# One wait per pair of write-backs, and the last store's wait in a section of its own: a row maximum over NaN data on one core

## The chip, the cores and the metric

The kernel runs on one core of one Trainium2 chip. The metric is the device time of a whole execution in microseconds (us); lower is better. The profile's span is some 1.8 us shorter than that time.

## The reference

```python
def setup_inputs():
    batch, seq, dim = 32, 2048, 2048
    x = np.random.randn(batch, seq, dim).astype(np.float32)
    mask = np.random.rand(batch, seq, dim) < 0.1
    x[mask] = np.nan
    return {"x": x, "axis": -1}

def reference(x, axis):
    return np.nanmax(x, axis=axis).astype(np.float32)
```

536.87 MB go in, 65,536 row maxima come out. A tenth of the elements are NaN and must not count.

## The kernel before

SyncE loads tiles of up to seven rows per partition into three large buffers. For each piece of a tile, ScalarE makes a 16-bit key from the upper half of every float (`kt`), a key in which NaN sorts low. GpSimd, or for a few pieces ScalarE (the negative numbers in `TILES`), writes the key back over the upper half (`xt`). VectorE then reduces whole rows with `tensor_reduce`. Each engine has a semaphore that it raises once per instruction, and `Order.add` works out which of them an instruction has to wait for. Where there are several, all but the last become wait instructions of their own:

```python
    def add(self, who, engine, issue, deps, lane=None, step=1):
        want = self.needed(who, deps)
        for s, v in want[:-1]:
            engine.wait_ge(self.sems[s], v)        # a separate wait instruction
        inst = issue()
        for s, v in want[-1:]:
            inst._wait_ge(self.sems[s], v)         # the wait on the instruction
        ...
# in the loop over the pieces of a tile:
                        if back:                   # ScalarE writes this piece back
                            held.append((at - c, at, key, kp, e_key))
                            ...
                        else:                      # GpSimd does
                            e = pool([e_key], out=to, in0=kp, scalar1=-1.0, ...)
                            kfree[key].append(e)
                            clean.append((at - c, at, e))
                        while reds and done + reds[0] <= ...:
                            ...
                            e = dve([e for a, b, e in clean if b > lo and a < done] + part,
                                    nc.vector.tensor_reduce, ...)
# ... at the end, inside the one critical section that holds the whole kernel:
        for (og, bits), e in zip(stores, ready):
            last = order.add("sp", nc.sync, lambda: nc.sync.dma_start(out=og, in_=bits), [e], ...)
        nc.sync.wait_ge(order.sems[last[0]], last[1])
```

The last tile, number 74 by the kernel's count, is cut into nine loads and seven maxima of one row each, so that little work is left after the last load.

## Time and profile before

| | before |
|---|---|
| time, median of the first three runs | 1253.67 us |
| span | 1251.8 us |
| read from HBM | 536.87 MB, 429 GB/s over the span |
| busy share: VectorE, GpSimd, ScalarE | 89%, 93%, 79% |
| separate waits on VectorE | 18 |
| last store landed to end of span | 1.28 us |

The prediction below shows the lines of the page, of a table of windows, of the chain of waits and of the source lines. In the table of windows the columns are the stretch, its length, the busy time of the engines with counts of instructions, the clock, the share of the 16 DMA engines' time that was busy, and GB/s.

### The profile page before, as it was taken

What the parts mean: (1) busy time and instruction counts of PE and PEld (TensorE: products, weight loads), DVE (VectorE), ACT (ScalarE), POOL (GpSimd) and SP (SyncE); (2) the same over time, 40 slices, a digit from 0 to 9 for tenths busy, and PEclk for the clock granted to TensorE, in tenths of its full rate; (3) what the DMA queues carried; (4) which work ended last, traced back from release to release, by engine and by line L of the source; (5) the groups of instructions that cost most, each with busy time, mean ns of one, the idle gap of its engine ahead of it and who ended that gap; (6) DMA issues with size and microseconds to landing.
All of it is one profiled execution on the core that took longest, in us unless ns stands there. A gap on an engine that the chain in (4) does not pass through costs nothing.

```text
span 1251.8 us, 892 instructions
## 1 busy us (share of the span) xinstructions
DVE 1110.9 (89%) x181; ACT 986.9 (79%) x273; POOL 1168.4 (93%) x242
## 2 busy tenths in 40 slices
DVE  0788989888889988898988888998888899999998
ACT  3777887778787877788777877777777878999998
POOL 2999989998999899998999899999999999989997
DMA  9999999999999999999999999999999999999997
GB/s 415 436 418 436 440 440 436 422 433 440 440 434 423 433 440 440 436 425 429 440 440 438 425 427 440 440 438 429 423 440 440 435 434 421 437 428 431 431 428 288
DMA packets 15991, 537.20 MB, mean 429 GB/s; under 512 B 2544, under 2 KB 2544, under 8 KB 3568
## 3 DMA queue, kind: packets, MB, share of 16 engines
q1 hardware_dynamic: 15984, 537.14, 99.3%
q14 instruction: 7, 0.06, 0.0%
HBM read 536.87 MB, written 0.26 MB: 429 GB/s over the span
## 4 chain that ended last, share of the span: by engine, by line
DMA 36%; DVE 33%; POOL 19%; ACT 10%; SPq 1%; issue 1%; DVEq 0%
DMA xt<-in_x_dram 36%; DVE acc L195 33%; POOL xt L191 19%; ACT kt L187 9%; ACT xt L187 1%; SPq L253 1%; DVE none L201 0%; DVE acc L215 0%; SPq L411 0%; DVEq L124 0%; SPq L183 0%
## 5 line engine op out<-in xcount | busy, mean ns | idle before, releaser
L191 POOL TENSOR_SCALAR xt<-kt 128x3584 int16<-128x3584 uint16 (+11 forms) x236 | 1167.4, 4946 | 78.5 <-ACT kt L187 60.3
L195 DVE TENSOR_REDUCE acc<-xt 128x3 f32<-128x6144 f32 (+4 forms) x175 | 1107.7, 6380 | 137.1 <-POOL xt L191 129.2
L187 ACT ACTIVATE kt<-xt,scalars 128x3584 uint16<-128x3584 int16 (+9 forms) x247 | 935.5, 3825 | 257.8 <-DMA xt<-in_x_dram 241.8
L187 ACT ACTIVATE xt<-kt 128x512 int16<-128x512 uint16 (+6 forms) x24 | 52.8, 2200 | 0.7
L187 ACT ACT_TABLE_LOAD x1 | 1.3, 1283 | 0.9 <-SPq L183 0.9
L195 DVE TENSOR_REDUCE xt<-xt 128x1 f32<-128x1536 f32 x1 | 1.7, 1742 | 0.0
L221 DVE MEMSET scalars<- 128x1 f32 x1 | 0.1, 59 | 1.0 <-SPq L183 1.0
L201 DVE TENSOR_SCALAR none<-acc 128x414 int32<-128x414 f32 (+1 forms) x2 | 0.8, 380 | 0.1
L215 DVE TENSOR_TENSOR acc<-acc,none 128x414 int32<-128x414 int32 (+1 forms) x2 | 0.7, 374 | 0.1
L201 POOL TENSOR_SCALAR late<-acc 128x91 int32<-128x91 f32 x1 | 0.5, 545 | 0.1
L215 POOL TENSOR_TENSOR acc<-acc,late 128x91 int32<-128x91 int32 x1 | 0.3, 343 | 0.1
L397 POOL MEMSET const-float32-0.0<- 128x1 f32 x1 | 0.1, 98 | 0.2 <-issue 0.2
L187 ACT ACTIVATE scalars<-scalars 128x1 f32<-128x1 f32 x1 | 0.2, 203 | 0.0
L397 POOL MEMSET const-uint8-127<- 128x1 uint8 x1 | 0.1, 102 | 0.0
L397 POOL MEMSET const-bfloat16-1.0<- 128x1 bf16 x1 | 0.1, 101 | 0.0
L397 POOL MEMSET const-float32-1.0<- 128x1 f32 x1 | 0.1, 98 | 0.0
## 6 DMA issues: line engine op xcount, KB each, us to landing
xt<-in_x_dram SPq DMA_DIRECT2D x61, 7168.0 KB, 22.5
xt<-in_x_dram SPq DMA_DIRECT2D x2, 5120.0 KB, 17.3
xt<-in_x_dram SPq DMA_DIRECT2D x3, 2816.0 KB, 22.5
xt<-in_x_dram SPq DMA_DIRECT2D x4, 2048.0 KB, 22.1
xt<-in_x_dram SPq DMA_DIRECT2D x5, 1536.0 KB, 28.9
xt<-in_x_dram SPq DMA_DIRECT2D x2, 3584.0 KB, 24.5
xt<-in_x_dram SPq DMA_DIRECT2D x6, 1024.0 KB, 26.7
xt<-in_x_dram SPq DMA_DIRECT2D x3, 1792.0 KB, 29.8
```

The lines of the kernel that those rows point to most:

```text
L187: return order.add("act", nc.scalar, lambda: nc.scalar.activation(**kw), deps)
L191: "pool", nc.gpsimd, lambda: nc.gpsimd.tensor_scalar(**kw), deps
L195: return order.add("dve", nc.vector, lambda: do(**kw), deps)
L201: lambda: engine.tensor_scalar(out=none, in0=acc, scalar1=NONE, scalar2=float(0x00800000), op0=ALU.is_equal, op1=ALU.mult,),
L215: lambda: engine.tensor_tensor(out=bits, in0=bits, in1=none, op=op),
L221: e_top = order.add("dve", nc.vector, lambda: nc.vector.memset(top, EDGE), [])
L253: lambda: nc.sync.dma_start(out=xt[:, at : at + c], in_=xg[:, base + at : base + at + c]),
L397: nc = _bacc.Bacc("TRN2", target_bir_lowering=False, num_devices=1)
```

## The change

There are two intents. First, where a maximum needs a write-back of GpSimd and one of ScalarE last, both raise one semaphore of that pair, and VectorE waits once. Second, the wait for the last store goes to a critical section that only SyncE enters, so that the engines' closing round runs while the store is in flight.

```diff
+APART = (70, 71, 72, 73)
+def joints(pieces, reds):
+    ...                      # which pieces are the last two, one of each engine, of a maximum
 ...
         inst.then_inc(self.sem(name), step)
 ...
+        past = self.past.get((name, event[1] - step), {}) if joint else {}
 ...
-        def pool(deps, **kw):
+        def pool(deps, pair=None, **kw):
             return order.add(
-                "pool", nc.gpsimd, lambda: nc.gpsimd.tensor_scalar(**kw), deps
+                "pool", nc.gpsimd, lambda: nc.gpsimd.tensor_scalar(**kw), deps,
+                lane=pair, joint=pair is not None,
             )
 ...
+                if number not in APART:
+                    pairs = joints(pieces, [n // Q for n in reds])
 ...
+                def cleaned(a, b, k, i, e):     # a piece counts when both of its pair are done
+                    ...
 ...
+    with tc.tile_critical():
         nc.sync.wait_ge(order.sems[last[0]], last[1])
```

(The same is done for `act`. `APART` lists four tiles that are left as they were.) In the built program VectorE's separate waits go from 18 to 8, ScalarE's from 14 to 18, and SyncE gains a few at the end.

## The prediction

> **What bounds the kernel now.** I read the page first, then a table of windows over the last fifth, then the chain of waits, and last the source lines of the two kinds of wait that change. From the page:
>
> ```profile
> span 1251.8 us, 892 instructions
> ...
> DVE 1110.9 (89%) x181; ACT 986.9 (79%) x273; POOL 1168.4 (93%) x242
> ...
> DMA  9999999999999999999999999999999999999997
> ...
> HBM read 536.87 MB, written 0.26 MB: 429 GB/s over the span
> ```
>
> All three compute engines are busy, but only the DMA row is full from the first slice to the 39th: 536.87 MB have to be read, and the span is mostly the time of that. The page's chain gives DVE 33% and GpSimd 19%; that is no contradiction, since a load is issued when VectorE frees a buffer and then waits in a queue that is already full. The windows over the last fifth show it (window, its length, busy us of VectorE, ScalarE, GpSimd with counts, clock, DMA share, GB/s):
>
> ```profile
> 1060.00:1140.00 80.00, 79.93 (x14) 76.85 (x25) 73.03 (x16) 1.00 0.99 429
> 1140.00:1200.00 60.00, 59.97 (x18) 57.05 (x24) 57.50 (x19) 1.00 1.01 431
> 1200.00:1235.00 35.00, 34.97 (x18) 33.67 (x24) 33.31 (x17) 1.00 1.01 425
> 1235.00:1240.00 5.00, 4.50 (x3) 4.92 (x4) 3.89 (x4) 1.00 1.02 425
> 1240.00:1245.00 5.00, 5.00 (x3) 4.94 (x6) 4.67 (x5) 1.00 0.41 146
> 1245.00:1252.00 7.00, 4.04 (x4) 1.28 (x2) 2.21 (x3) 1.00 0.04 7
> ```
>
> The DMA share stays at about 1.0 until 1240 although VectorE is also at 79.93 of 80 us. So a reduction that starts a little earlier before 1240 frees a buffer a little earlier for a transfer that only queues longer. After 1240 the loads are over (by the trace's records the last lands at 1243.20), and the end is set by this stretch of the chain of waits (start us, us, what):
>
> ```profile
> 1213.18 23.03 DMA xt<-in_x_dram
> ...
> 1236.24 1.58 ACT kt L187
> 1237.82 0.07 issue
> 1237.89 1.92 POOL xt L191
> 1239.81 0.03 issue
> 1239.84 2.01 DVE acc L195
> 1241.84 0.20 issue
> 1242.04 2.06 DVE acc L195
> ...
> 1244.23 2.15 DVE acc L195
> ...
> 1246.42 2.29 DVE acc L195
> ```
>
> A load lands at 1236.21, is turned into keys, written back, and the fourth row maximum of the last tile starts at 1239.84. From there four maxima follow back to back, starting 2.20, 2.19 and 2.19 us apart, though the intervals have waits of pairs in them. The waits themselves:
>
> ```profile
> L124 DVEq EVENT_SEMAPHORE  x18: 21/21/21, 158.1 to 1246.4; - x18
> ...
> L183 SPq COMPARE_BRANCH  x1: 38/38/38, 1250.5 to 1250.5; - x1
> ...
> L183 POOLq DRAIN  x1: 41/41/41, 1250.8 to 1250.8; - x1
> L183 DVEq DRAIN  x1: 17/17/17, 1250.8 to 1250.8; - x1
> ...
> L183 SPq NOP  x1: 18/18/18, 1251.0 to 1251.0; - x1
> ```
>
> The first line is the extra wait instruction that VectorE runs before a maximum that needs two engines: 18 in the whole kernel. The others are the round at the end: SyncE branches 0.02 us after the last store has landed (1250.53), then ScalarE, GpSimd and VectorE drain, and SyncE collects their answers until its NOP at 1251.02.
>
> **What the skill says.** The Trainium skill, "Perfetto Trace Analysis", section "Identifying Dependency Chains": an instruction that waits for several engines may have EventSemaphore instructions put before it. The trace agrees: 18 of them on VectorE. The same page, "Per-instruction lifecycle", under "DVE / Act Engine Instruction": an instruction with its own wait stands in a hardware wait queue, pushed there ahead of time, while under "Sequencer-only Instruction" the sequencer fetches the next one only after its own wait is over. So a separate wait should cost something only when it is the last to be met. The trace agrees. The third maximum of the last tile starts 110 ns after GpSimd's end (1236.938 to 1237.048) through the separate wait, the fourth 35 ns after it (1239.801 to 1239.836) with the wait on itself: a late separate wait costs about 75 ns. On DMA, "DMA: Bandwidth & Descriptors", section "Anatomy of one DMA", says that the fixed cost is mostly the write receipt before the semaphore; here the last store, 3.5 KB, takes 1.40 us from issue to landing (1249.13 to 1250.53), and neither kernel can shorten that.
>
> **The change, part by part.** The order of instructions on each engine shows that no computation and no transfer moves. What moves:
>
> *Pairs.* In ten maxima (tiles, counted from 1, 9, 17, 25, 33, 41, 63, 66, 67, 68 and the fifth of the last tile) the two waits become one, on a semaphore that both write-backs raise; VectorE's separate waits go from 18 to 8. In three more maxima of the last tile (third, sixth, seventh) the separate wait stays, but is for an earlier piece. ScalarE gains four waits (14 to 18), in tiles 63, 66, 67 and 68. The upper bound is 13 times 75 ns, 0.98 us, if every one were late and on the path. They are not:
> - In the five early tiles the maximum waits up to 1.6 us for ScalarE's write-back, a wait that stands on the instruction itself already; the separate one, for GpSimd, is met 0.4 us before the start (in the one at 293.83, the wait was over at 293.42). Gain 0.
> - Tile 63: separate wait ends at 1065.295, start 1065.339, 68 ns after the maximum before had ended. Gain up to 0.07 us on VectorE, but the DMA queue is full then, and VectorE has 0.50 us of idle time later, before 1239.84, that is set by a landing. Gain at the end 0.
> - Tiles 67 and 68: separate waits end 0.40 and 1.48 us before the start. Gain 0.
> - Last tile: the third maximum could start 44 ns earlier (back to back would be 1234.811 + 2.193 = 1237.004), and this vanishes in the same 0.50 us. The fifth starts 2.203 us after the fourth where plain neighbours are 2.193 apart: 0.01 us, and this one counts. The sixth and seventh are 2.192 and 2.193 apart: 0, but they can follow the fifth, as their last write-back ends at 1246.317, over 0.1 us before the start at 1246.424.
> Sum at the end: 0.01 us.
>
> *The last wait.* In before, landing to SyncE's arrival at the closing barrier takes 1250.528 to 1251.157, 0.63 us: branch, the semaphore for the others, three drains, two collecting waits, a NOP, a drain. In the changed kernel the round with the three engines follows the issue of the store and lies inside its 1.06 us of flight (1249.465 to 1250.528); it needed 0.45 us (1250.583 to 1251.034). But the second section brings its own: after the landing a wait, a branch, a semaphore, a drain that waits for it, a NOP that waits for the drain, and the closing drains, all on SyncE. From intervals of before, as an estimate: wait seen 0.017 and run 0.028, step to the branch 0.044, branch 0.038, step after it 0.127, semaphore 0.017, step 0.074, drain 0.007, step 0.060, NOP 0.018, step 0.044, drain 0.007, step 0.056: sum 0.54 us. Saved: 0.63 - 0.54 = 0.09 us. The barrier after it has the same instructions.
>
> Total 0.01 + 0.09 = 0.10 us: 1253.67 - 0.10 = 1253.57, given as 1253.55.
>
> **Rivals.** (1) *The whole round is saved.* If the second section's own steps are mostly merged or run ahead, all of 0.45 us goes: 1253.2. For it: branches without a wait are not seen in the trace at all, so some steps may vanish. Against: the second section's branch carries a wait, and such a branch was seen, with 0.127 us after it. (2) *The new section takes the place of the old.* If the added instructions at the end have to be fetched anew, or each step costs more than in before, the end is 0.1 to 0.3 us later: 1253.8 to 1254.0. For it: more waits and another branch on SyncE. Against: most of them run during the store's flight. (3) *The pairs matter upstream.* If an earlier release of a buffer shortened the loading, up to 1 us could go: 1252.6. For it: VectorE is at 100% from 1060 on. Against: the DMA share of 0.99 to 1.01 there, and loads that land 17 us or more after their issue. (4) *ScalarE's four new waits hurt:* at most 4 x 0.075 = 0.3 us in tiles 63 to 68. ScalarE is at 76.85 of 80 us there, so it has room, and the 0.50 us at 1239.3 would swallow the rest.
>
> **Range and chances.** The three runs of before lie 0.2 us apart, which is twice the expected gain, so the measured difference may come out as nothing. Rival 1 sets the lower end at about 1253.15, rival 2 and drift between runs the upper at about 1253.95. Two per cent is 25 us; nothing here touches that, so within 2% gets 0.99.
>
> **What would show it.** Right: VectorE's separate waits 8 in place of 18 and ScalarE's 18 in place of 14; busy times of the engines and the loads' landings as before within their noise; the last four maxima 2.19 us apart; from the last store's landing to the end of the span about 1.19 us where before has 1.28 (1251.81 - 1250.53). Wrong: the load before the fourth last maximum landing at clearly another time than 1236.2, which would make loading the cause; landing to end shortened by 0.3 us or more (rival 1), or lengthened (rival 2).

## More of the kernel before

One line that the prediction did not show turns out to matter. It is in the list of DMA queues between 1225 and 1245 us (queue and kind: packets, MB, share of 16 engines):

```profile
q1 hardware_dynamic: 1812, 7.06, 86.2%
q14 instruction: 1, 0.01, 0.1%
```

Beside the 1812 packets of loads and stores, one packet of 8 KB carries instructions. Over the whole span there are seven such packets.

## The result

The changed kernel took 1253.16 us (median of six runs, 1253.02 to 1253.23) against 1253.72 us for the kernel before (six runs, 1253.66 to 1253.86), so 0.56 us less. The ratio is 0.9995. Ratios are the mean time of one kernel's runs over that of the other's of the same rounds, so not quite the ratio of the medians. The 95% interval, 0.9982 to 1.0008, holds 1. The six times of the one do not overlap the six of the other, and in two later sessions the same kernel came out 0.75 and 0.71 us under before. A gain of 0.5 to 0.75 us is therefore real, but it is 0.05% of the time.

The page of the changed kernel:

```profile
span 1251.3 us, 893 instructions
...
DVE 1110.9 (89%) x181; ACT 986.8 (79%) x273; POOL 1169.5 (93%) x242
...
DMA  9999999999999999999999999999999999999997
...
HBM read 536.87 MB, written 0.26 MB: 429 GB/s over the span
```

Busy times and the DMA row are those of before. The windows at the end, with the same columns:

```profile
1235.00:1240.00 5.00, 5.00 (x4) 5.00 (x4) 4.62 (x4) 1.00 1.02 426
1240.00:1245.00 5.00, 5.00 (x3) 4.93 (x6) 4.68 (x5) 1.00 0.39 136
1245.00:1252.00 7.00, 3.61 (x4) 0.77 (x1) 1.70 (x3) 1.00 0.04 8
```

VectorE is busy for all 5.00 us between 1235 and 1240, where before it was for 4.50. The half microsecond of idle time ahead of the fourth-last maximum is gone. The timeline of VectorE shows the same, first of before, then of the changed kernel (start us, us, engine and line, operation, shape, count, and in brackets the idle time before it and what ended it):

```profile
1239.84 8.87 DVE L195 TENSOR_REDUCE acc<-xt 128x1 f32<-128x2048 f32 x4 [0.50 <-POOL xt L191]
```

```profile
1232.81 15.47 DVE L243 TENSOR_REDUCE acc<-xt 128x1 f32<-128x2048 f32 x7
```

Before, the last four maxima are a group of their own behind a gap; now all seven of the last tile are one group. The chain of waits of the changed kernel agrees (start us, us, what):

```profile
1235.86 1.34 POOL xt L236
1237.20 0.02 issue
1237.22 5.54 DVE acc L243 x3
1242.77 1.04 issue
```

It no longer goes through a landing at 1236.21. By the trace's records the load in question now lands at 1235.64, 0.57 us earlier, although the loads up to 1230 land 0.19 us later than before. The change of 0.75 us happens at one load: a 512 KB load that landed 1.98 us after its predecessor now lands 1.23 us after it. It was not issued earlier (at 1210.47 in place of 1210.28), so an earlier release of its buffer is not the reason. The fourth-last maximum starts at 1239.43 in place of 1239.84, and the last store lands at 1250.13 in place of 1250.53.

What sits in that place is the packet of instructions. The DMA queues of the changed kernel, first between 1225 and 1245 us (where before had two kinds of packets), then between 1245 and the end:

```profile
q1 hardware_dynamic: 1808, 7.03, 85.6%
```

```profile
q1 hardware_dynamic: 288, 0.05, 3.7%
q14 instruction: 1, 0.01, 0.3%
```

The trace's records put the packet at 1231.70 us before and at 1245.62 us now. The last load lands at 1243.06, so the packet now comes after all of them.

The source lines of the waits, as the prediction showed them for before:

```profile
L158 DVEq EVENT_SEMAPHORE  x8: 21/21/21, 1181.6 to 1244.4; - x8
...
L219 SPq NOP  x1: 18/18/18, 1249.4 to 1249.4; - x1
...
L493 SPq EVENT_SEMAPHORE  x5: 17/17/464, 1249.6 to 1251.2; - x5
...
L493 SPq COMPARE_BRANCH  x1: 38/38/38, 1250.2 to 1250.2; - x1
```

VectorE has 8 separate waits. SyncE's round with the others ends with its NOP at 1249.4, during the store's flight, where before it ended at 1251.0. From the landing (1250.13) to the end of the span (1251.28) it is 1.15 us, where before had 1.28.

So the 0.53 us of the two profiled spans (1251.81 and 1251.28) are 0.13 us at the end and 0.40 us in the landing of the last store, and the latter come from a load.

### The profile page after: what moved, and what is told of

It is laid out like the page before. It is cut to its first block, busy times and chain, and to the rows that moved or that the text cites. A ratio compares the mean times of both kernels' runs of the same rounds, so it can differ in the third digit from the quotient of the medians.

```text
span 1251.3 us, 893 instructions
## 1 busy us (share of the span) xinstructions
DVE 1110.9 (89%) x181; ACT 986.8 (79%) x273; POOL 1169.5 (93%) x242
## 4 chain that ended last, share of the span: by engine, by line
DMA 38%; DVE 27%; POOL 20%; ACT 13%; issue 1%; SPq 0%; ACTq 0%
DMA xt<-in_x_dram 38%; DVE acc L243 27%; POOL xt L236 20%; ACT kt L226 11%; ACT xt L226 2%; SPq L307 0%; DVE none L249 0%; DVE acc L263 0%; SPq L493 0%; ACTq L158 0%; SPq L219 0%
```

## The theories

**Fetch theory.** VectorE's program is fetched in blocks as it runs. Ten wait instructions fewer put the last fetch of that stream behind the last load in place of among the last loads, and the loads are no longer held up by it. The Trainium skill, "Runtime: NRT & Kernel Launch", section "Instruction fetch mechanics", says that each sequencer fetches its next page by DMA while it executes the current one, and calls the cost mostly hidden; "DMA: Bandwidth & Descriptors", section "Queues, rings and completion order", gives queue row 14 to the runtime's own traffic, refills among it. The trace agrees with the mechanism: seven packets of 8 KB on queue 14 in both kernels. By "Perfetto Trace Analysis", section "The 4-stage abstract model", an instruction has 64 bytes; as an estimate from that, one packet is 128 instructions. ScalarE had started 48 and 175 instructions at two of the packets of before, GpSimd 52 and 180 at two others: 127 and 128 apart. VectorE had started 189 at the last packet in both kernels, at 1231.70 and at 1245.62. Its other packet does not show the same step: by these counts it comes 133 instructions before the last one in before (56 at 434.2 us) and 142 in the changed kernel (47 at 385.7). So the count alone does not lay the packet to VectorE's stream, and the trace does not name its owner; the experiments have to.

**Wait theory.** The separate waits themselves were late and held up the maxima; with fewer of them VectorE, and through it the loads, run earlier.

**Section theory.** The end section alone makes the gain.

## The experiments

In all of them the result was correct. Times are medians of five runs, "before" is the kernel before in the same rounds (nine runs). Each call used one chip, and before's medians differ between them by up to 0.25 us, so only differences within a call are compared. The intervals of the ratios (about plus or minus 0.13%, 1.6 us) are wider than all these differences; what is read are medians that hang together over runs, and the traces. The five runs of one version lie 0.2 to 1.0 us apart, so a difference of 0.1 or 0.2 us between medians is not resolved. The profiled run is one of the five and not always a typical one: for pairs alone and for six waits it was the fastest, for the section alone and for nine waits the slowest. Starts of maxima are therefore not compared across versions to the tenth; what is compared is what happens inside a trace.

### The two parts alone

Pairs alone: the changed kernel without its second section.

```diff
-
-    with tc.tile_critical():
         nc.sync.wait_ge(order.sems[last[0]], last[1])
```

> The change without its second section: pairs alone, the last store's wait back where it was. Fetch theory (the pairs take ten instructions from VectorE's stream, so that its last instruction fetch falls after the last load in place of among the last loads): the 8 KB packet on the instruction queue is at about 1245.6 us, the fourth-last maximum starts near 1239.4, saving about 0.42 us: 1253.30. Section theory (the end alone accounts for it): no saving, 1253.72. Landing of the last store to the end of the span as before, 1.28 us.

Measured: 1253.30 us against 1253.66, 0.36 less (single runs 1252.95 to 1253.39). The packet is at 1245.4, there is no gap before the fourth-last maximum, which starts at 1239.18, and landing to end is 1.28 us. The section theory falls as the whole explanation.

The section alone: the kernel before with the one line `with tc.tile_critical():` added.

```diff
+
+    with tc.tile_critical():
         nc.sync.wait_ge(order.sems[last[0]], last[1])
```

> The kernel before with the second section alone. Fetch theory: the fetch stays at about 1231.7 us, loads and maxima as before; only landing to end goes from 1.28 to 1.15 us: about 1253.59, saving 0.13. Section theory: saving about 0.5 us, 1253.2.

Measured: 1253.51 us against 1253.66, 0.15 less. The packet is at 1232.1, the gap is there (0.34 us), and landing to end is 1.15 us. The two parts sum to 0.51 us, close to the 0.56 of the whole, though 0.15 us is within the spread of single runs; the trace's 1.28 to 1.15 us after the landing is the firmer number.

### The pairs kept, the length of the stream put back

The changed kernel with nine more wait instructions on VectorE at the start, each already satisfied (17 waits in the source, which the build merges in twos):

```diff
         act([e_top], out=warm, in_=top, func=ACT.Prelu, alpha=0.5)
+        for _ in range(17):
+            nc.vector.wait_ge(order.sems[e_top[0]], e_top[1])
```

> The changed kernel with nine satisfied wait instructions on VectorE at the start, where it is idle for 9 us: the pairs stay as they are, the length of the stream is what before had. Fetch theory: the last fetch is back at about 1231.7, the loads after it land about 0.5 us later, the fourth-last maximum waits for a landing again: about 1253.58, 0.42 over the changed kernel. Wait theory (fewer separate waits, so earlier maxima, made the gain): it stays at 1253.16.

Measured: 1253.71 us against 1253.66 for before. The gain is gone, although all pairs are in place. Its timeline of VectorE has the gap again:

```profile
1240.08 8.87 DVE L243 TENSOR_REDUCE acc<-xt 128x1 f32<-128x2048 f32 x4 [0.77 <-POOL xt L236]
```

The packet is at 1231.8, and the 512 KB load lands 2.20 us after its predecessor. This speaks against the wait theory plainly: no wait of a maximum differs from the changed kernel, only the number of instructions ahead. That the section's 0.15 us are not seen in this time (0.05 over before in place of 0.15 under) is of the size of the spread.

### The waits of the last tile, and all others

Pairs in every tile but the last, then pairs in the last alone:

```diff
-                if number not in APART:
+                if number not in APART and number < 74:
```

```diff
-                if number not in APART:
+                if number == 74:
```

> The changed kernel with pairs in every tile but the last, so that the five maxima at the end wait as in before; nine of the ten waits are still gone from VectorE's stream, all of them ahead of the last tile. Fetch theory: the last fetch still falls after the loads (about 1243 to 1246), the whole gain is kept: about 1253.15. Wait theory (the gain comes from the waits of the last tile, the only ones near the end): the gain is lost, about 1253.55.

> The converse: pairs in the last tile alone. VectorE's stream ahead of the last loads is as long as in before. Fetch theory: the last fetch stays near 1231.7, the fourth-last maximum waits for a late landing, only the section's 0.13 to 0.15 is gained: about 1253.52. Wait theory: about 1253.15.

Measured, against 1253.56 us for before: 1252.84 with pairs in all but the last tile (0.72 less; one of the five runs was at 1253.73), and 1253.51 with pairs in the last alone (0.05 less). The timelines, of the first and of the second:

```profile
1234.89 13.29 DVE L243 TENSOR_REDUCE acc<-xt 128x1 f32<-128x2048 f32 x6
```

```profile
1239.82 8.87 DVE L243 TENSOR_REDUCE acc<-xt 128x1 f32<-128x2048 f32 x4 [0.53 <-POOL xt L236]
```

The packets are at 1246.9 and at 1231.7. As far as five runs each can tell, the whole gain of the pairs comes from tiles whose waits were far from the end, and none from those that stand in the tail. Only the count of instructions ahead of the last loads is common to the good versions.

### A dose in between

The same edit as for nine waits, with six.

> The changed kernel with six satisfied waits on VectorE at the start: the last fetch should come when the separate wait of the third maximum of the last tile has passed (1235.8), so at about 1237 to 1239.5 us, before the last two or three loads only. Fetch theory: those loads alone land 0.4 to 0.75 us late, the load that the fourth-last maximum needs does not; about 0.2 us slower than the changed kernel, 1253.35, between it and the nine-wait version. Wait theory: 1253.16.

Measured: 1253.18 us against 1253.56, between the two versions above (0.34 over the one, 0.33 under the other). The packet is at 1239.3; the second-last load lands 2.55 us after its predecessor in place of 1.84, the ones before are on time, and the fourth-last maximum has no gap. The delay moved to the load that follows the packet, as said. That the time lies in between is not resolved: the five runs range from 1252.99 to 1253.68 us. In the trace, of the fastest of them, the delay costs 0.11 us of idle time before the last maximum.

### The fetch moved far ahead

The kernel before with 60 more satisfied waits on VectorE (119 in the source).

> The kernel before with 60 satisfied wait instructions on VectorE at the start: its last fetch moves from 1231.7 to about 1020 us, still among the loads. If a fetch costs the loading the same wherever it falls (lag that is kept): 1253.7, as before. If a fetch is made up for unless it falls among the last loads: about 1253.3. Wait theory: 1253.7 too, so this run alone does not tell it from the first.

Measured: 1253.76 us against 1253.66. The list of DMA queues between 915 and 925 us has the packet now:

```profile
q1 hardware_dynamic: 93, 4.42, 102.3%
q14 instruction: 1, 0.01, 0.2%
```

It came at 921 us, not at 1020 as estimated, and the stream's first fetch came at 11.5 us in place of 434 (there the load that landed at 23.4 came 17.6 us after its predecessor in place of 16.9). The last loads are on time among themselves (the 512 KB load takes 1.23 us) and the gap is gone, but the load in whose interval the packet fell took 17.88 us in place of 16.90, and from 1060 to 1230 every load lands about 0.66 us later than before. So it is not the place among the last loads that costs. The loading held this delay through its second-last load; the last one landed at 1243.12, about where it did in before (1243.20) and in the changed kernel (1243.06). A fetch can cost wherever loads are queued; behind the last load it costs nothing.

The landings of the steady phase show the same in the two first profiles. Big loads land 16.86 to 16.97 us apart, except in these intervals (from the trace's records; landing at its end, interval, packets in it):

```
before   259.8  17.01  (248.1, 254.6)     after   259.9  17.36  (246.2, 254.6)
before   446.1  17.33  (434.2)            after   395.4  17.28  (385.7)
before   953.5  17.12  (939.8)            after   953.8  17.33  (940.1)
before  1004.3  17.07  (999.1)            after  1004.4  16.89  (999.2)
```

And at the end, for the 512 KB load that lands near 1233:

```
kernel                       packet at   load after its predecessor   gap before 4th-last maximum
before                        1231.7            1.98 us                    0.50 us
section alone                 1232.1            1.83                       0.34
pairs + 9 waits               1231.8            2.20                       0.77
pairs in the last tile only   1231.7            1.98                       0.53
before + 32 on ScalarE        1232.2            1.76                       0.25
changed                       1245.6            1.23                       0
pairs alone                   1245.4            1.24                       0
pairs in all but the last     1246.9            1.24                       0
```

(The row with 32 waits on ScalarE is a run of the next section.)

### Other engines' fetches

If the fetches of VectorE cost, those of the others might too. The changed kernel with 32 satisfied waits on ScalarE (63 in the source):

```diff
         act([e_top], out=warm, in_=top, func=ACT.Prelu, alpha=0.5)
+        for _ in range(63):
+            nc.scalar.wait_ge(order.sems[e_top[0]], e_top[1])
```

> The changed kernel with 32 satisfied wait instructions on ScalarE at the start, where it waits 3.7 us for the first load; VectorE's stream is untouched. ScalarE's fetches should move 32 instructions earlier (940 to about 760 us), and a third one may come near 1222 us, among the last loads. Fetch theory: if it comes, loads after it land 0.4 to 0.75 us late and the time is about 1253.5; if no third one comes, 1253.16. Wait theory: 1253.16 in both cases.

Measured: 1252.68 us against 1253.56, the lowest time of all, which neither theory had said. ScalarE's packets had moved, to 68 and 762 us, and a third came at 1240.0, which did not reach the load that the fourth-last maximum needs. The landings near 73 and 767 were on time (16.89 and 16.98 us). I read this as: ScalarE's and GpSimd's fetches cost when they fall close together. Three runs tested that, on another chip: half the waits on ScalarE; 32 waits on GpSimd in place of ScalarE (`nc.gpsimd.wait_ge` in the same loop); and 32 waits on ScalarE in the kernel before.

> The changed kernel with 16 satisfied waits on ScalarE at the start, half of the 32 that came out about 0.4 us faster than the changed kernel: ScalarE's fetches at about 155 and 850 us, far from GpSimd's at 254 and 999, and no third one. Spread theory (two fetches near each other hold up the loads by about 0.4 us, one alone by 0.0 to 0.2): the landing after 254 is no longer 0.4 us late, about 1252.7. If the 32 waits gained by their number or their third fetch: about 1253.1, like the changed kernel.

> The same the other way round: 32 satisfied waits on GpSimd at the start of the changed kernel, which moves GpSimd's fetches to about 75 and 820 us and leaves ScalarE's at 247 and 940. Spread theory: about 1252.7 again. If it was ScalarE's own fetches that cost: about 1253.1.

> The kernel before with 32 satisfied waits on ScalarE at the start, no pairs and no second section. VectorE's fetch stays at about 1231.7, among the last loads. Spread theory: about 0.4 us under before, 1253.2, although nothing of the change is in it; if the tail's late landing swallows it (VectorE back to back is not the limit there): 1253.2 as well, as the whole loading is earlier. If the gain needs the changed tail: 1253.6.

The changed kernel itself ran beside them.

> The changed kernel itself, for the spread between sessions and as the base of the three others: about 1253.15, 0.45 to 0.55 under before, its last VectorE fetch at about 1245.6.

Measured, against 1253.81 us for before: 1253.17, 1253.02 and 1253.78, and 1253.06 for the changed kernel itself. None gains anything over its base. In the last of the three (the kernel before with ScalarE's packets at 68.6 and 762.4, as in the fast run) the two intervals took 17.21 and 17.26 us. The idea of fetches that are spread out fell.

The fast version was then repeated beside the changed kernel.

> The changed kernel with 32 satisfied waits on ScalarE, a second time. If the 0.4 us belong to the kernel (ScalarE's fetches at 68 and 762 us cost the loading nothing): about 0.4 us under the changed kernel of the same call, its 63rd load landing about 0.35 us earlier. If they belonged to that session, or to where its instructions lay in memory: the same as the changed kernel within 0.15 us.

> The changed kernel a third time, as the base of the run beside it: about 1253.1, 0.5 to 0.75 under before.

Measured: 1253.21 us for it and 1252.95 for the changed kernel, against 1253.66 for before. The gain did not come again; the version is, if anything, slower. Its traces say where: ScalarE's packets came at 68.6 and 762.4 us as in the fast run (68.2 and 762.0), but the landings after them took 17.24 and 17.32 us, and after the third packet, at 1240.4, the last load landed 2.96 us after its predecessor (2.43 in the changed kernel beside it), with 0.18 us of idle time before the last maximum. The 1252.68 belonged to that session: the version with pairs in all but the last tile, of the same session, was low as well at 1252.84. I know no version that beats the changed kernel.

## Why the prediction was wrong, point by point

- **"The order of instructions on each engine shows that no computation and no transfer moves."** This is the step that failed. It is true of the transfers that the program issues; the transfer of the program itself moves, from 1231.7 to 1245.6 us, because VectorE has ten instructions fewer. The packets were in the page of before, in its list of queues ("instruction: 7"), and I had not read that line.
- **"Sum at the end: 0.01 us" for the pairs.** In its place the runs show 0.36 us for the pairs alone, and 0.67 us (1253.51 minus 1252.84) between pairs in the last tile alone and pairs in all the others, which moves the packet from 1231.7 to 1246.9. As far as waits go the sum was right: the fifth maximum gained 0.011 us (2.203 to 2.192), the third 0.016 us, and a version with all the waits paired and the stream at its old length gains nothing.
- **"Tiles 67 and 68: separate waits end 0.40 and 1.48 us before the start."** A misreading: these are tiles 66 and 67. In tile 68 the wait ended 44 ns before the start (1140.869 and 1140.913), as late as in tile 63, and it is missing in the sum. It makes no difference that the runs show: the version with all the waits paired and nine waits added gains nothing.
- **"So a reduction that starts a little earlier before 1240 frees a buffer a little earlier for a transfer that only queues longer."** Right. It is why rival 3, with up to 1 us from pairs upstream, stays wrong in its mechanism although its direction came true.
- **The 0.50 us before 1239.84, "set by a landing".** Right, and it was the place to look at: that landing was late by the 0.75 us that the load before it had lost. I took it for given, and used it as a cushion that swallows gains elsewhere.
- **The last wait, 0.09 us.** Right in mechanism and a little small: 0.13 us by the traces (1.28 to 1.15), 0.15 us by the run of that part alone. From landing to SyncE's arrival at the barrier it took 0.50 us where the sum said 0.54. Rivals 1 and 2 did not happen.
- **ScalarE's four new waits.** No harm seen; ScalarE is busy 76.81 of 80 us from 1060 to 1140, as before (76.85).
- **What would show it wrong:** "the load before the fourth last maximum landing at clearly another time than 1236.2, which would make loading the cause". This is what happened: 1235.64.

In total I had 0.10 us (written as 1253.55, so 0.12 under 1253.67); it was 0.56. The direction, the end and the waits were right; the missing term is the fetch, 0.41 us at the fourth-last maximum in the two profiles. The time itself, 1253.16, lies just above the low end of the range, 1253.15, which rival 1 had set for another reason.

**What one fetch costs.** The records of single DMA packets in the traces give the size. Take the five profiles with a packet near 1232 us (before, section alone, pairs + 9 waits, pairs in the last tile only, before + 32 waits on ScalarE). The packet takes 0.31 us. The data packet that starts as it ends and another that starts 0.35 us later, of 4 KB each, take 0.37 and 0.49 us in place of 0.16. That makes 0.85 us in all. Each load's records end with sixteen packets of 4 bytes, read here as one for each DMA engine. In these five profiles fifteen of the sixteen of the 512 KB load come 1.24 to 1.26 us after those of the load before, and one comes 2.08 us after; in the changed kernel, in pairs alone and in pairs in all but the last tile all sixteen come after 1.24 to 1.26. So one engine of sixteen loses 0.83 us, and the load lands when the last engine is done. How late that is depends on where the hit engine stood: with nine waits it was the last of the sixteen before the packet too, and the landing was 0.97 us late; in before + 32 on ScalarE it was 0.45 us ahead of the last, and the landing was 0.53 us late.

The steady phase shows the same. After the packet at 921 the hit engine was the last one, and the landing was 0.98 us late. At 1004.4 in the changed kernel a fetch took 0.53 us from an engine that was 0.65 us ahead of the last, and the landing was on time. The two sessions with 32 waits on ScalarE differ in this too. Near 74 and 767 us the fetches took 0.56 us from an engine in both, but in the fast one these engines were 0.77 and 0.68 us ahead of the last, in the repetition 0.33 and 0.26. So part of that session's low time was luck.

The same records name the owner. In the steady phase, too, the data packet after a fetch is slow. After the packets that move when waits are added to VectorE it takes 0.53 to 0.54 us more than others of its size, after those that move with ScalarE's waits 0.24 to 0.25, and with GpSimd's 0.22. The packet near 1232 or 1245 us moves with VectorE's waits alone (none, 6 and 9 of them: 1245.6, 1239.3, 1231.8; with 32 on ScalarE or on GpSimd it stays at 1245.5 to 1245.8), and where loads follow it, it has VectorE's 0.54.

**What stays open.** Why data packets after a fetch are slow, and more so after VectorE's, the runs do not show. Nor do they show why the landing came 0.45 to 0.47 us after the last 4-byte packet where a fetch had hit, and 0.32 to 0.33 elsewhere. Which engine a fetch falls on and what sets how far each engine is ahead, the runs do not show either, so the cost of one fetch to a load, 0 to 1.0 us, can't be foretold from the kernel.

## What to carry to other kernels

In a kernel that keeps the DMA engines full, the instruction stream is a load too: count the instructions of each engine, find the instruction packets in the list of DMA queues, and see between which loads they fall. When a change only adds or removes waits and yet moves the time, look at where those packets went before crediting the waits; padding the stream with satisfied waits tells the two apart. Gains of this kind depend on a count and are lost by the next edit that adds a few instructions, so check them again at the end.

## What the Trainium skill lacked or had wrong

- "Runtime: NRT & Kernel Launch", section "Instruction fetch mechanics", gives refills of 16 KiB, 256 instructions, as mostly hidden. Here the packets during the run were of 8 KB, and ScalarE's and GpSimd's came 127 to 128 instructions apart by the trace's counts (VectorE's 133 and 142). Their cost is hidden from the engine that executes, but not from a saturated load stream: 0.4 us of later landings at VectorE's packet in the steady phase (17.33 and 17.28 us in place of 16.90), and 0.5 to 1.0 us at the end (1.76 to 2.20 in place of 1.23), where each took 0.83 us from one DMA engine.
- "Perfetto Trace Analysis", "Per-instruction lifecycle", says for sequencer-only instructions that the recorded time leaves the semaphore wait out. A wait instruction with two conditions was recorded with 464 ns (the line with 17/17/464 above), until 0.02 us after the landing it waited for, so at least part of its wait is in the record.
- "Perfetto Trace Analysis", section "Identifying Dependency Chains", names the separate waits for several engines but no cost. Here one cost about 75 ns more than a wait on the instruction when it was the last to be met (110 against 35 ns), and nothing when it was met early.
